# A transformer and expert block on one core: an unused 352-byte tile in the pool of norms

## The chip, the core and the metric

The kernel runs on one core of a Trainium2 chip. The metric is the time of one execution in device microseconds. A core has a matrix engine (TensorE, PE in the profile), a vector engine (DVE), a scalar engine (ACT), GpSimd (POOL), and queues that issue transfers (SP above all). PE reads both operands of a matmul from the on-chip memory SBUF and writes its result to PSUM. One operand, the stationary one, is loaded into the array first (LDWEIGHTS, PEld in the profile); the other, the moving one, is streamed through it column by column (MATMUL). SBUF has 128 partitions; a tile has the same byte address in each of them, so "address" below means the byte in a partition.

## The reference

512 tokens of width 1024 go through two blocks, in float32. What matters here is the first one: four gated feed-forward layers (FFN) with a state-space mixer after the first and a latent attention after the third.

```python
def swiglu(h, w_gate, w_up, w_down):
    return (jax.nn.silu(h @ w_gate) * (h @ w_up)) @ w_down

for i in range(DEPTH):                      # DEPTH = 2
    x = x + 0.5 * swiglu(rms_norm(x, norm_w[i, 0]), ...)
    x = x + (mamba2_mixer if i % 2 == 0 else mla_mixer)(rms_norm(x, norm_w[i, 1]), ...)
    x = x + 0.5 * swiglu(rms_norm(x, norm_w[i, 2]), ...)
```

The hidden width of an FFN is 2816. The second block (a mixer of three kinds of heads, then 16 routed experts) follows on the result.

## The kernel before, in words

All activations lie transposed: a tile is 128 features by 512 tokens, 2048 bytes in each partition. Every float32 value is held as two parts, high and low, in the format float32r, and each product is three matmuls (`mm3`, lines 176 to 181): high weights by high activations (L179), high weights by low activations (L180), low weights by high activations (L181). Names in the profile are `out<-moving,stationary`. With 512 tokens the moving operand has 512 columns, and the stationary one is a block of 128 columns, 512 bytes wide, of a weight tile.

Weights come from memory into two buffers `raw` (9216 bytes each, pool `rawp`), and ACT and DVE split them into `wh` and `wl` (pool `wp`, three buffers of 4608 bytes of each).

An FFN works in two halves of 12 and 10 hidden blocks (`FF_HALVES`). In the gate and up products (`products`, result `ps_p`) the moving operands are `xh` and `xl`, the split norm input, in pool `xw`. The hidden blocks are split into `hh` and `hl` (pool `fact`, line 295), and the down product (`row_matmul`, `row_steps`, result `ps_d`) streams these. The state-space mixer ends in the same `row_steps` with 16 tiles `ghi`/`glo`: the first eight were put into pool `xw` (line 365), the last eight into a pool `shp` of their own (line 374). The attention ends in `row_steps` with tiles `oh`/`ol`, all in `xw`. PE's program is written out by hand (`manual_schedule`); within `row_steps` it takes six matmuls for one result before it goes to the next:

```python
for k in range(2):
    c = slice(k * 512 + d * P, k * 512 + (d + 1) * P)
    f = 2 * u + k
    self.mm3(pd[d], (w[0][:, c], w[1][:, c]), hs[f], f == 0, f == 2 * n - 1)
```

Pools lie one above the other in SBUF in the order in which they are opened. Open from the start of the first block to the end of the mixer are `cst`, `rawp`, `wp`, `xp` (the running sum x), `xw` and `nrm`, whose tiles hold the squares, the row sums and the reciprocal roots of the norms. Each stage opens its own pools above `nrm` and closes them at its end. Pools marked `side="right"` count down from the top, and the pools of the expert stage are opened after `nrm` has been closed. Where the pools named below start in the built programs, in bytes, with the rest after division by 512 in brackets:

| pool | holds | before | after |
|---|---|---|---|
| `cst` | constants; identity at 17632 (224) | 16512 (128) | the same |
| `wp` | `wh`, `wl` | 41888 (416) | the same |
| `xp` | x | 69536 (416) | the same |
| `xw` | `xh`, `xl`, first `ghi`, `glo`, `oh`, `ol` | 85920 (416) | the same |
| `nrm` | `ssq`, `sq`, `dg`, small columns | 118688 (416) | 119040 (256) |
| `fact` | `hh`, `hl` (28 tiles of 2048) | 145472 (64) | 145824 (416) |
| `shp` | last `ghi`, `glo` (16 tiles of 2048) | 157760 (64) | 158112 (416) |
| `st2` | convolved tiles of the mixer (`xT` among them) | 197824 (192) | 198176 (32) |
| `mt3` | attention probabilities | 216064 (0) | 216416 (352) |
| `how` | output weights of the second mixer, from the right | 179232 (32) | the same |
| `et3` | rows of the expert stage | 134048 (416) | the same |

Since the tiles of `wp`, `xw`, `fact` and `shp` are multiples of 512 bytes, the rest in brackets is that of each tile in the pool, and of each weight block.

Of the kernel before, what the change touches and what calls it, by code (L numbers as in the profile page):

```python
# [7 lines left out]
F32 = mybir.dt.float32  # L8
# [10 lines left out]
P = 128  # L19
# [107 lines left out]
class Kern:  # L127
# [10 lines left out]
    def open_features(self, ctx):  # L138

        self.wp = self.pool(ctx, "wp", 3)  # L140
        self.xp = self.pool(ctx, "xp")
        self.xw = self.pool(ctx, "xw")
        self.nrm = self.pool(ctx, "nrm")

    def pool(self, ctx, name, bufs=1, side=None):
        return ctx.enter_context(self.tc.tile_pool(name=name, bufs=bufs, reuse_waits="tile", side=side))
# [2006 lines left out]
```

## Time and profile before

| | |
|---|---|
| median of three runs | 2694.84 us (2693.6 to 2697.28) |
| profiled execution | 2697.9 us, span from first to last instruction 2696.0 us |
| PE busy | 2602.4 us, 97% of the span, 12798 matmuls |
| DVE, ACT, POOL busy | 1553.2, 1059.9, 230.5 us |
| share of PE in the chain that ended last | 86% |
| mean granted PE clock | 0.981 of 2.4 GHz |

Busy times of matmuls overlap: each is recorded from its start to its modelled end, and the next one starts before that. What a matmul costs on a full PE is therefore the distance from its start to the next one's, not its own duration. The profile shows no addresses; those above are read from the programs.

### The profile page before, as it was taken

The numbers are of one execution on the slowest core, as the hardware profiler recorded it, in microseconds if no ns is written. First come the engines' busy times: TensorE is split into PE (matmuls) and PEld (weight loads), VectorE is DVE, ScalarE is ACT, GpSimd is POOL, SyncE is SP. The second block draws the span as 40 slices with busy tenths as digits, with TensorE's granted clock in tenths as the row PEclk, the third lists the DMA queues.
The fourth block names the chain that finished last, engine by engine and source line by source line (L and its number), as shares of the span: only waits on it lengthen the run. The fifth ranks groups of instructions, "written<-read, shape, count | busy, mean of one in ns | idle before, by whom it ended". The sixth has DMA issues, their size and how long they took to land.

```text
span 2696.0 us, 32260 instructions
## 1 busy us (share of the span) xinstructions
PE 2602.4 (97%) x12798; PEld 2144.4 (80%) x12798; DVE 1553.2 (58%) x2609; ACT 1059.9 (39%) x1789; POOL 230.5 (9%) x172
## 2 busy tenths in 40 slices
PE   8999999999999999999999999999999989997996
PEld 6888887888888888888888887888888878766774
DVE  5434357676766454657534367645434364767997
ACT  4322235645443222333322236643322234534674
POOL 0000001111110000000000003200000001303332
PEclk9999998999999999999999999999999989988998
DMA  4222321212134242534422222002222222115796
GB/s 153 94 94 97 106 83 62 79 63 79 63 134 149 102 160 96 183 130 146 167 94 94 94 85 78 17 23 104 94 94 98 106 84 92 48 40 188 254 338 197
DMA packets 57048, 300.77 MB, mean 112 GB/s; under 512 B 12066, under 2 KB 12578, under 8 KB 27706
## 3 DMA queue, kind: packets, MB, share of 16 engines
q1 hardware_dynamic: 49232, 281.21, 29.8%
q0 software_dynamic: 5328, 11.59, 1.5%
q10 hardware_dynamic: 2330, 5.84, 0.6%
q8 instruction: 102, 1.67, 0.2%
q14 instruction: 56, 0.46, 0.0%
HBM read 290.68 MB, written 15.75 MB: 114 GB/s over the span
## 4 chain that ended last, share of the span: by engine, by line
PE 86%; DVE 8%; DMA 3%; ACT 2%; issue 1%; SPq 0%; ACTq 0%; POOL 0%; DVEq 0%; POOLq 0%
PE ps_p L179 12%; PE ps_p L180 12%; PE ps_p L181 12%; PE ps_d L179 8%; PE ps_d L180 8%; PE ps_d L181 8%; PE ps_in L179 3%; PE ps_in L181 3%; PE ps_in L180 3%; DVE wl L167 3%; DMA expert_out<-ey,edst 2%; PE ps_s L833 1%; PE ps_o L859 1%; PE ps_y L541 1%; PE ps_z L180 1%
## 5 line engine op out<-in xcount | busy, mean ns | idle before, releaser
L166 ACT CAST wh<-raw 128x1024 fp32r<-128x1024 f32 (+3 forms) x494 | 485.6, 994 | 1130.7 <-PE ps_p L180 378.3
L167 DVE TENSOR_TENSOR wl<-raw,wh 128x1024 fp32r<-128x1024 f32 (+3 forms) x494 | 574.7, 1175 | 374.6 <-ACT wh L166 365.2
L179 PE MATMUL ps_p<-xh,wh 128*128 128x512 f32 x1408 | 550.2, 391 | 6.7 <-ACT xh L172 6.7
L180 PE MATMUL ps_p<-xl,wh 128*128 128x512 f32 x1408 | 550.0, 391 | 0.6 <-DVE xl L173 0.6
L181 PE MATMUL ps_p<-xh,wl 128*128 128x512 f32 x1408 | 549.4, 390 | 0.0
L179 PEld LDWEIGHTS ps_p<-xh,wh 128*128 128x128 f32 x1408 | 265.6, 189 | 62.7 <-ACT xh L172 6.7
L180 PEld LDWEIGHTS ps_p<-xl,wh 128*128 128x128 f32 x1408 | 265.3, 188 | 57.0 <-DVE xl L173 2.0
L181 PEld LDWEIGHTS ps_p<-xh,wl 128*128 128x128 f32 x1408 | 265.3, 188 | 55.3
L179 PE MATMUL ps_d<-hh,wh 128*128 128x512 f32 x704 | 279.1, 397 | 0.0
L181 PE MATMUL ps_d<-hh,wl 128*128 128x512 f32 x704 | 279.1, 396 | 0.0
L180 PE MATMUL ps_d<-hl,wh 128*128 128x512 f32 x704 | 279.1, 396 | 0.0
L294 DVE TENSOR_TENSOR h<-ps_p,g 128x512 f32<-128x512 f32 x88 | 60.8, 690 | 230.2 <-PE ps_p L181 229.8
L291 DVE TENSOR_TENSOR g<-ps_p,rb 128x512 f32<-128x512 f32 x88 | 60.3, 689 | 177.6 <-PE ps_p L181 177.6
L181 PEld LDWEIGHTS ps_d<-hh,wl 128*128 128x128 f32 x704 | 132.6, 188 | 32.3
L180 PEld LDWEIGHTS ps_d<-hl,wh 128*128 128x128 f32 x704 | 132.6, 188 | 32.3
L179 PEld LDWEIGHTS ps_d<-hh,wh 128*128 128x128 f32 x704 | 132.6, 188 | 32.2
L179 PE MATMUL ps_in<-xh,wh 128*128 128x512 f32 x336 | 140.9, 419 | 0.7 <-ACT wh L166 0.7
L181 PE MATMUL ps_in<-xh,wl 128*128 128x512 f32 x336 | 132.4, 394 | 0.5 <-DVE wl L167 0.5
L180 PE MATMUL ps_in<-xl,wh 128*128 128x512 f32 x336 | 132.1, 393 | 0.0
L181 PEld LDWEIGHTS ps_in<-xh,wl 128*128 128x128 f32 x336 | 63.6, 189 | 15.1 <-DVE wl L167 1.0
L962 DVE SCALAR_TENSOR_TENSOR macc<-mraw,c_act,macc 128x1024 f32<-128x1024 f32 x42 | 53.9, 1284 | 36.8 <-DMA mraw<-w_mod 36.2
L179 PEld LDWEIGHTS ps_in<-xh,wh 128*128 128x128 f32 x336 | 63.9, 190 | 12.9 <-ACT wh L166 1.1
(581 smaller groups left out, 4151.4 us busy)
## 6 DMA issues: line engine op xcount, KB each, us to landing
raw<-w_ffn SPq DMA_DIRECT2D x131, 1024.0 KB
raw<-w_moe SPq DMA_DIRECT2D x48, 1024.0 KB
raw<-w_ssm SPq DMA_DIRECT2D x31, 1024.0 KB
mraw<-w_mod SPq DMA_DIRECT2D x48, 512.0 KB
raw<-w_hyb SPq DMA_DIRECT2D x9, 1024.0 KB
expert_out<-zero SPq DMA_DIRECT2D x8, 512.0 KB
raw<-w_mla SPq DMA_DIRECT2D x4, 1024.0 KB
xtok<-expert_out POOLq DMA_DIRECT2D x8, 512.0 KB, 9.5
```

Source lines behind the costliest of these rows:

```text
L166: a = self.nc.scalar.copy(hi, src)
L167: b = (eng or self.nc.vector).tensor_sub(lo, src, hi.bitcast(F32))
L179: mm(out, ah, bh, start=start, stop=False)
L180: mm(out, ah, bl, start=False, stop=False)
L181: mm(out, al, bh, start=False, stop=stop)
L291: nc.vector.tensor_mul(g, pg, r)
L294: nc.vector.tensor_mul(h, pu, g)
L541: nc.tensor.matmul(py[:, blk(h, 64)], G[h][:, c], xdt[:, 4 * c + h], start=True, stop=True)
L833: nc.tensor.matmul(ps[:, :n], t["qT"][:, blk(i)], t["kT"][:, :n], start=True, stop=False)
L859: nc.tensor.matmul(t["po"][:, blk(i, 64)], t["pT", i][:, blk(j)], v[:, j, h], start=j == 0, stop=j == i)
L962: nc.vector.scalar_tensor_tensor(acc, w, ca[:, k:k + 1], acc, op0=ALU.mult, op1=ALU.add)
```

## The change

One line opens a tile in `nrm` that nothing reads or writes.

```diff
@@ open_features
         self.xp = self.pool(ctx, "xp")
         self.xw = self.pool(ctx, "xw")
         self.nrm = self.pool(ctx, "nrm")
+        self.nrm.tile([P, 88], F32, name="pad")
```

88 float32 are 352 bytes in each partition. The tile is the first that is taken from `nrm`, so it lies at the start of that pool: the other tiles of `nrm` move by 352 bytes too, and so does every pool opened above it while it is open (the pools of the four FFNs, of both mixers and of the modulation). Pools below it, those from the right and those of the expert stage stay where they are. The instructions of the two programs are the same, in the same order, with the same waits, on all five engines; only addresses differ.

## Rows read from the trace of the kernel before

**Rows 1.** The page: engines over the span; the chain by engine and line.

```profile
PE 2602.4 (97%) x12798; PEld 2144.4 (80%) x12798; DVE 1553.2 (58%) x2609; ACT 1059.9 (39%) x1789; POOL 230.5 (9%) x172
...
PE 86%; DVE 8%; DMA 3%; ACT 2%; issue 1%; SPq 0%; ACTq 0%; POOL 0%; DVEq 0%; POOLq 0%
PE ps_p L179 12%; PE ps_p L180 12%; PE ps_p L181 12%; PE ps_d L179 8%; PE ps_d L180 8%; PE ps_d L181 8%; PE ps_in L179 3%; PE ps_in L181 3%; PE ps_in L180 3%; DVE wl L167 3%; DMA expert_out<-ey,edst 2%; PE ps_s L833 1%; PE ps_o L859 1%; PE ps_y L541 1%; PE ps_z L180 1%
```

**Rows 2.** Matmuls by tile: duration min/median/max in ns, first and last start.

```profile
L179 PE MATMUL ps_p<-xh,wh x1408: 387/389/797, 6.7 to 2143.9; 128*128 128x512 f32 x176
...
L179 PE MATMUL ps_d<-hh,wh x704: 392/397/483, 148.9 to 2201.0; 128*128 128x512 f32 x176
...
L180 PE MATMUL ps_d<-hl,wh x704: 392/397/400, 149.1 to 2201.3; 128*128 128x512 f32 x176
...
L179 PE MATMUL ps_d<-ghi,wh x128: 387/394/987, 756.1 to 854.6; 128*128 128x512 f32 x128
...
L179 PE MATMUL ps_d<-oh,wh x64: 389/389/481, 1789.1 to 1835.7; 128*128 128x512 f32 x64
```

**Rows 3.** Windows: engines busy (x instructions touching the window), clock, DMA.

```profile
core 0: us, PE busy (x) PEld busy (x) DVE busy (x) ACT busy (x) POOL busy (x), PEclk, DMA share, GB/s
150.00:216.00 66.00, 66.00 (x283) 53.04 (x283) 23.48 (x27) 12.07 (x12) 0.00 (x0) 1.00 0.23 80
220.00:324.00 104.00, 104.00 (x460) 86.17 (x459) 41.82 (x47) 30.22 (x38) 0.00 (x0) 1.00 0.29 98
789.50:809.50 20.00, 20.00 (x87) 16.09 (x86) 11.95 (x15) 6.15 (x9) 0.00 (x0) 1.00 0.85 307
812.00:832.00 20.00, 20.00 (x90) 16.57 (x89) 16.03 (x17) 7.40 (x10) 0.00 (x0) 1.00 0.63 220
834.50:854.50 20.00, 20.00 (x87) 16.10 (x86) 8.18 (x14) 5.48 (x11) 0.00 (x0) 1.00 0.23 88
1803.00:1836.00 33.00, 33.00 (x147) 27.33 (x146) 17.89 (x27) 13.20 (x22) 0.00 (x0) 1.00 0.28 93
```

**Rows 4.** Timeline of PE: first and last matmul in five of these windows.

```profile
149.81 0.40 PE L180 MATMUL ps_d<-hl,wh 128*128 128x512 f32 x1
...
215.89 0.39 PE L180 MATMUL ps_d<-hl,wh 128*128 128x512 f32 x1
...
219.77 0.39 PE L179 MATMUL ps_p<-xh,wh 128*128 128x512 f32 x1
...
323.81 0.39 PE L179 MATMUL ps_p<-xh,wh 128*128 128x512 f32 x1
...
789.22 0.39 PE L179 MATMUL ps_d<-ghi,wh 128*128 128x512 f32 x1
...
809.37 0.40 PE L181 MATMUL ps_d<-ghi,wl 128*128 128x512 f32 x1
...
811.71 0.39 PE L179 MATMUL ps_d<-ghi,wh 128*128 128x512 f32 x1
...
831.88 0.39 PE L181 MATMUL ps_d<-ghi,wl 128*128 128x512 f32 x1
...
1802.79 0.40 PE L181 MATMUL ps_d<-oh,wl 128*128 128x512 f32 x1
...
1835.89 0.39 PE L180 MATMUL ps_d<-ol,wh 128*128 128x512 f32 x1
```

**Rows 5.** Waits: who waited for whom, us in total, times, longest us.

```profile
ACT wh L166 <- PE ps_d L180: 344.4, 92, 8.8
```

**Rows 6.** Matmuls with the identity as moving operand, by tile, columns as in rows 2.

```profile
L1540 PE MATMUL ps_hT<-squares,hg x120: 270/272/328, 2497.0 to 2646.5; 128*128 128x128 f32 x120
L845 PE MATMUL ps_pT<-squares,prb x112: 270/273/330, 1673.1 to 1792.9; 128*128 128x128 f32 x112
L511 PE MATMUL ps_x<-squares,xT x64: 270/272/273, 442.0 to 759.5; 128*128 128x128 f32 x64
```

**Rows 7.** Output product of the second mixer, by tile, columns as in rows 2.

```profile
L179 PE MATMUL ps_out<-ow,yh x32: 389/396/483, 2427.5 to 2460.4; 128*128 128x512 f32 x32
```

**Rows 8.** Span and mean granted clock of the core.

```profile
core 0: 2696.0 us, clock 0.981
```

## The prediction

> **What bounds the kernel now.** The page comes first: PE is busy for 97% of the span, and 86% of the chain that ended last is PE [rows 1]. Products of one form, 128x512 float32r, fill most of it: by line the chain is ps_p three times 12% and ps_d three times 8%. A change that moves only addresses can change the time in two ways, by what a single instruction takes or by who meets whom at a memory, and on this kernel either must show on PE to count.
>
> So the second view is the tiles. All 1408 x 3 products ps_p have a median of 389 ns [rows 2]. The FFN's down products stream the same 512 columns against the same weight tiles, and have 397 ns (704 x 3 of them). The attention's output product, which runs through the same `row_steps` lines as these, has 389 ns. The state-space mixer's, through `row_steps` again, has 394 ns, which lies between. The code that issues them is not what makes 397 of 389.
>
> Durations overlap, so the third view gives the distance from start to start: windows in which PE never pauses, with the count of matmuls that touch them [rows 3], and the first and last of these on the timeline [rows 4]. In the FFN's down product 283 matmuls make 282 steps from 149.81 to 215.89 us: 66.08 / 282 = 234.3 ns. In the following up product 459 steps from 219.77 to 323.81 give 226.7 ns. In the attention's output 146 steps from 1802.79 to 1835.89 give 226.7 ns. The granted clock is 1.00, that is 2.4 GHz, in all of them.
>
> The mixer's output decides what the difference hangs on. By the order of `row_steps` each of its two quarters takes 96 matmuls on the eight tiles in `xw`, then 96 on the eight in `shp`. The window 789.5 to 809.5 lies on `shp`: 86 steps in 20.15 us, 234.3 ns. The window 812 to 832 lies on `xw`: 89 steps in 20.17 us, 226.6 ns. The window 834.5 to 854.5 lies on `shp` again, with the count of the first, 87 against 90. One stage, one set of lines, one clock, three windows, and the step follows the pool of the moving tile. It does not follow the load: DMA moved 307, 220 and 88 GB/s in the three, and DVE and ACT were busier in the second than in the others [rows 3].
>
> What differs between the pools is their start. Weights and `xw` have the rest 416 after division by 512; `fact` and `shp` have 64. Every 512-column product above at 226 to 227 ns has operands with equal rests; those at 234 ns have a distance of 160 between them (64 - 416 + 512).
>
> **The change, part by part.** No instruction is added, removed or moved past another, so there is no queue or wait to price, only addresses.
>
> Tiles of `fact` and `shp` go from 64 to 416, the rest of the weights that they meet. The FFNs have 704 x 3 = 2112 such matmuls. The mixer has 128 x 3 = 384, half of them, 192, on `shp`. Each should take 226.7 in place of 234.3 ns: 2112 x 7.6 ns = 16.1 us, and 192 x 7.6 ns = 1.5 us, together 17.5 us. From below the gain is bounded by nothing at all (if the rest is not what counts), from above by this sum, since no 512-column stretch that I timed runs under 226.6 ns. I take the whole sum, because two windows already show `row_steps` at 226.6 and 226.7 ns when the rests agree, and after the change the relation is the same one.
>
> Does it reach the end? In these windows PE is busy without a gap (66.00 of 66.00, 20.00 of 20.00), and ps_d is 24% of the chain. The next thing that could be late is weights. ACT waits for ps_d 92 times, 344.4 us in all, for a weight buffer to come free [rows 5]; it stands ahead of PE. A pair of split weight tiles feeds 24 matmuls in the up product as in the down product, and the up product holds 226.7 ns over 104 us with 98 GB/s of transfers and no gap [rows 3]. The down product then asks for the same rate, so the cover suffices.
>
> The tiles of `nrm` move too, from 416 to 256. They feed PE in 14 products that spread a norm over the rows and in some sums of one column; at the 7.6 ns seen above the 14 would cost 0.1 us. I take nothing.
>
> The remaining products with one moved operand are mostly transposes: about 620 whose moving operand is the identity, which stays, while the turned tile moves. Those of `hg` (rest 416), `prb` (0) and `xT` (192) have medians of 272, 273 and 272 ns [rows 6]. Three rests give one duration, so I take nothing; if each lost 7.6 ns it would be 4.7 us. Products of which both operands move keep their distance. DVE, ACT and POOL have slack in the stages that I sum, and the transfers into moved tiles feed work beside them. I take nothing for these either.
>
> The sum is -17.5 us. The profiled execution took 2697.9 us, which is 3.1 us above the median of the three runs; it goes to 2680.4, and the median from 2694.8 to **2677.3 us**. The three runs differ by 3.7 us, and the mean clock of 0.981 [rows 8] says that some stretches run at 1.2 GHz; an earlier end of a stage can make such a stretch a little longer or shorter. For the likeliest case alone I therefore give 2672 to 2683.
>
> **The rivals.** First, nothing changes: 2694.8 us. The address table allows another reading of the same rows: every moving tile at 227 ns lies below byte 118688 and every one at 234 above 145000. If the place counts and not the rest, `fact` and `shp` stay as high as they are and keep their 234 ns. One row leans against it, without force: the `how` tiles lie at 179232 and up, as high, with the rest 32, and their product has 396 ns in one of its three lines, broken up by other work [rows 7]. It would also come out so if the second operand cost nothing at any address and something else in the two pools held them back. The Trainium skill speaks for no change: SBUF — State Buffer, section "Who interferes with whom", has it that PE never waits on anyone for SBUF, and TensorE: Matmul & The Clock Gate, section "Step-by-step: what each phase is for", says "Loading the next tile's weights doesn't steal SBUF read bandwidth from the running matmul." By these pages an address costs nothing and the sum is zero; the two windows of one stage, 234.3 and 226.6 ns, do not agree with that. I give this rival 7 in 100.
>
> Second, half the gain: rests by a larger number than 512 count as well, and only part of the blocks meet well. The tiles of `fact` have 416 by 2048 then, those of `xw` 1952. Against it: in ps_p the eight weight blocks of a tile lie 512 bytes apart, so eight distances by 2048 and more occur, and the window of 104 us has one step throughout. The time would be about 2686. I give 4 in 100.
>
> Third, slower. Moved tiles start at a multiple of 64 bytes before and 32 bytes past one after. If a moving operand wants a start at a multiple of 64 and `xw` is fast for another reason, the down products get worse. The row of `hl` shows 400 ns as the longest [rows 2], 3 ns above the median; a step that grew by as much on 2304 matmuls would give 6.9 us, and with half of what the transposes could lose at the utmost some 9: about 2704. It decides the sign once the mean step in these stretches passes 236.6 ns (5.4 us over 2304). Against it stand the 4224 matmuls ps_p, which start 32 past a multiple of 64 and are the fastest. I give 4 in 100.
>
> **How the numbers follow.** The likeliest case has 85 in 100. What three runs can tell from no change is about 0.2%, 5.4 us. The likeliest and the half gain are faster by more: 0.89. The first rival is the same: 0.07. The third is slower: 0.04. The range reaches from just under the likeliest case to past the half gain, 2671 to 2688; outside it are the first and third rivals and a little of the likeliest, under 2 in 10.
>
> **What would show it.** In the profile after, the median of `hh` and `hl` falls from 397 to 389 ns, and that of `ghi` from 394 to 389. A gapless 66 us of the FFN's down product is touched by some 292 matmuls in place of 283. The three windows on the mixer's output have the same count. Each FFN's first down half (288 matmuls) is 2.2 us shorter, its second (240) 1.8 us, and the up products, the attention and the experts take what they took. I am wrong if the step of the down product stays at 234 (then the place counts, or what is in the pools), or if it falls and the end does not come earlier, by a new gap on PE or more time at 1.2 GHz.

## The result and the profile after

The changed kernel takes 2676.11 us (median of 6 runs, 2673.09 to 2677.55), the kernel before 2694.68 us on the same chip (median of 6). The ratio is 0.9934, 95% interval 0.9923 to 0.9945. That is 18.6 us less, where 17.5 were forecast (2677.3 us), and lies inside the range of 2671 to 2688.

The page of the profiled execution after the change (2677.55 us, span 2675.6) begins and ends its chain with these lines. They answer to [rows 1]; all line numbers of the code have grown by one.

```profile
PE 2580.3 (96%) x12798; PEld 2139.8 (80%) x12798; DVE 1552.2 (58%) x2609; ACT 1060.3 (40%) x1789; POOL 229.2 (9%) x172
...
PE 86%; DVE 9%; ACT 2%; DMA 1%; issue 1%; SPq 0%; ACTq 0%; POOL 0%; DVEq 0%
PE ps_p L180 12%; PE ps_p L182 12%; PE ps_p L181 12%; PE ps_d L180 8%; PE ps_d L181 8%; PE ps_d L182 8%; DVE wl L168 3%; PE ps_in L180 3%; PE ps_in L182 3%; PE ps_in L181 3%; PE ps_s L834 1%; PE ps_o L860 1%; PE ps_y L542 1%; PE ps_z L181 1%; PE ps_z L180 1%
```

The same 12798 matmuls keep PE busy for 22.1 us less, and DVE, ACT and POOL have not moved by more than 1.3 us. The same products lead the chain; the transfer `expert_out<-ey,edst`, 2% of it before, is no longer in this line. It belongs to the expert stage, behind everything that the sum counted.

The second view is the matmuls by tile, with minimum, median and maximum of the duration in ns, and the first and last start; it answers to [rows 2].

```profile
L180 PE MATMUL ps_p<-xh,wh x1408: 387/389/794, 6.8 to 2127.5; 128*128 128x512 f32 x176
...
L180 PE MATMUL ps_d<-hh,wh x704: 388/389/481, 148.6 to 2182.8; 128*128 128x512 f32 x176
...
L181 PE MATMUL ps_d<-hl,wh x704: 389/389/390, 148.8 to 2183.1; 128*128 128x512 f32 x176
...
L180 PE MATMUL ps_d<-ghi,wh x128: 387/389/987, 750.7 to 848.3; 128*128 128x512 f32 x128
...
L180 PE MATMUL ps_d<-oh,wh x64: 387/389/478, 1774.9 to 1821.5; 128*128 128x512 f32 x64
```

`hh`, `hl` and `ghi` have come down to the 389 ns that `xh` and `oh` had all along. The last start in a row is a clock for the whole of what was summed: all FFNs and the state-space mixer lie before the last `ps_d<-hh`. It started at 2201.0 us before [rows 2] and starts at 2182.8 now, 18.2 us earlier.

The third view is the windows, engines busy (x instructions touching the window), granted clock and DMA; it answers to [rows 3].

```profile
148.50:214.00 65.50, 65.50 (x291) 54.24 (x290) 24.63 (x28) 13.37 (x14) 0.00 (x0) 1.00 0.25 88
218.00:322.00 104.00, 104.00 (x461) 86.11 (x460) 41.82 (x47) 30.22 (x38) 0.00 (x0) 1.00 0.29 99
...
785.00:805.00 20.00, 20.00 (x90) 16.56 (x89) 12.31 (x16) 6.81 (x10) 0.00 (x0) 1.00 0.88 311
807.00:827.00 20.00, 20.00 (x89) 16.54 (x89) 16.42 (x17) 7.33 (x9) 0.00 (x0) 1.00 0.63 225
829.50:849.50 20.00, 20.00 (x90) 16.58 (x89) 8.70 (x18) 6.71 (x14) 0.00 (x0) 1.00 0.20 70
```

The down product of the first FFN half is gapless still (65.50 of 65.50), and 291 matmuls now touch a window that is half a microsecond shorter than the one that 283 touched. The up product behind it is as it was. In the three windows on the mixer's output the counts were 87, 90, 87; they are 90, 89, 90. The first and the last of the 288 matmuls of that down half, on PE's timeline:

```profile
148.57 0.39 PE L180 MATMUL ps_d<-hh,wh 128*128 128x512 f32 x1
...
213.62 0.39 PE L182 MATMUL ps_d<-hh,wl 128*128 128x512 f32 x1
```

287 steps in 65.05 us are 226.7 ns each, where [rows 4] gave 234.3.

### The profile page after: what moved, and what is told of

It reads as the page before. It is cut to its first block, busy times and chain, and to the rows that moved or that the text cites. A ratio compares the mean times of both kernels' runs of the same rounds, so it can differ in the third digit from the quotient of the medians.

```text
span 2675.6 us, 32260 instructions
## 1 busy us (share of the span) xinstructions
PE 2580.3 (96%) x12798; PEld 2139.8 (80%) x12798; DVE 1552.2 (58%) x2609; ACT 1060.3 (40%) x1789; POOL 229.2 (9%) x172
## 4 chain that ended last, share of the span: by engine, by line
PE 86%; DVE 9%; ACT 2%; DMA 1%; issue 1%; SPq 0%; ACTq 0%; POOL 0%; DVEq 0%
PE ps_p L180 12%; PE ps_p L182 12%; PE ps_p L181 12%; PE ps_d L180 8%; PE ps_d L181 8%; PE ps_d L182 8%; DVE wl L168 3%; PE ps_in L180 3%; PE ps_in L182 3%; PE ps_in L181 3%; PE ps_s L834 1%; PE ps_o L860 1%; PE ps_y L542 1%; PE ps_z L181 1%; PE ps_z L180 1%
## 5 line engine op out<-in xcount | busy, mean ns | idle before, releaser
L181 PE MATMUL ps_p<-xl,wh 128*128 128x512 f32 x1408 | 549.6, 390 | 0.6 <-DVE xl L174 0.6
L181 PEld LDWEIGHTS ps_p<-xl,wh 128*128 128x128 f32 x1408 | 265.3, 188 | 57.5 <-DVE xl L174 2.2
L181 PE MATMUL ps_d<-hl,wh 128*128 128x512 f32 x704 | 273.9, 389 | 0.0
L181 PEld LDWEIGHTS ps_d<-hl,wh 128*128 128x128 f32 x704 | 132.2, 188 | 27.4
L181 PE MATMUL ps_in<-xl,wh 128*128 128x512 f32 x336 | 131.3, 391 | 0.0
```

The lines of the kernel that those rows point to most:

```text
L181: mm(out, ah, bl, start=False, stop=False)
```

## The experiments

All kernels below issue the same instructions in the same order on each engine as the kernel before; they differ in addresses. Steps are distances between the starts of neighbouring matmuls on PE's timeline, as a mean over all of a kind that run without a pause. "Distance" is the start of the moving tile less that of the weight block, after division by 512.

**Only what lies above the norms moves.** The change also moves the tiles of `nrm`. Here the 352 bytes lie in a pool of their own above it, so that `nrm` stays.

```diff
         self.nrm = self.pool(ctx, "nrm")
+        self.pool(ctx, "padp").tile([P, 88], F32, name="padp")
```

> The 352 bytes stand in a pool of their own above the pool of norms, whose tiles stay at their old addresses; fact and shp start with the rest 416 as in the changed kernel. If the distance between moving tile and weights is the whole cause: ratio 0.993, about 2676 us, and a step of 226.7 ns in the down products. If the move of the norms' own tiles brought or cost a part: a ratio between 0.994 and 1.000, or under 0.992.

Measured: 2673.63 us, ratio 0.9932 (0.9915 to 0.9948), step of `ps_d<-hh` 226.6 ns.

```profile
L180 PE MATMUL ps_d<-hh,wh x704: 389/389/481, 148.3 to 2180.9; 128*128 128x512 f32 x176
```

The whole effect is there without the norms' own tiles.

**Everything from the weights up moves by 96 bytes.** Absolute places and remainders change, distances do not.

```diff
+        self.pool(ctx, "padp").tile([P, 24], F32, name="padp")
         self.wp = self.pool(ctx, "wp", 3)
```

> 96 bytes stand ahead of the weight pool, so that weights, xw, fact and shp all rise by 96: rests 0, 0, 160, 160. Every distance is that of before. If the distance counts: ratio 1.000, about 2695 us, ps_d<-hh 234.3 ns a step and ps_p 226.7. If the start of the moving tile alone counts (416 is good because it is 32 past a multiple of 64): the tiles of xw, at a multiple of 64 now, fall to about 234 (some 5600 matmuls, +40 us) and fact, 32 past one, rises to 227 (-17.5 us): about 2717 us.

Measured: 2693.78 us, ratio 1.000 (0.9991 to 1.001). The tile view of this kernel has the durations of before:

```profile
L180 PE MATMUL ps_p<-xh,wh x1408: 387/389/792, 6.6 to 2144.0; 128*128 128x512 f32 x176
...
L180 PE MATMUL ps_d<-hh,wh x704: 392/397/482, 148.8 to 2201.1; 128*128 128x512 f32 x176
```

Weights and `xw` start at a multiple of 512 here, `fact` and `shp` at 160 past one, and the two products keep their steps of 226.8 and 234.3 ns. Neither kind of start has a value by itself, which takes away the rival of starts at a multiple of 64.

**The fast tiles are moved off the weights.** 160 bytes ahead of `xw` give it the distance that `fact` had. 352 more above `nrm` keep `fact` and `shp` at 160.

```diff
         self.xp = self.pool(ctx, "xp")
+        self.pool(ctx, "padx").tile([P, 40], F32, name="padx")
         self.xw = self.pool(ctx, "xw")
         self.nrm = self.pool(ctx, "nrm")
+        self.pool(ctx, "padp").tile([P, 88], F32, name="padp")
```

> 160 bytes ahead of xw and 352 after it: xw has the rest 64 against 416 of the weights, fact and shp have 64 as before. If the distance counts, the products on xw get the step that fact had: ps_p 234.3 ns in place of 226.7 for 4224 matmuls, ps_in, the mixer's and the attention's outputs on xw for some 1400 more: +40 us, about 2735, ratio 1.015; ps_d<-hh keeps 234.3. If the 234 ns belong to the tiles of fact and shp for another reason than their start: ratio 1.000.

Measured: 2729.98 us, ratio 1.0141 (1.0124 to 1.0158), 35.6 us slower than before. The tile view (two lines of code are added, so L179 is L181 here), and a window of 62 us on a down product and one of 100 us on an up product:

```profile
L181 PE MATMUL ps_d<-hh,wh x704: 392/397/475, 152.2 to 2234.3; 128*128 128x512 f32 x176
...
L181 PE MATMUL ps_p<-xh,wh x1408: 391/397/792, 6.7 to 2177.2; 128*128 128x512 f32 x176
...
L181 PE MATMUL ps_d<-oh,wh x64: 392/397/481, 1813.2 to 1860.9; 128*128 128x512 f32 x64
```

```profile
153.00:215.00 62.00, 62.00 (x267) 49.83 (x266) 21.61 (x25) 11.30 (x12) 0.00 (x0) 1.00 0.25 86
220.00:320.00 100.00, 100.00 (x429) 80.39 (x428) 40.26 (x46) 27.79 (x35) 0.00 (x0) 1.00 0.29 98
```

`xw` still lies low, below 119 KB, and its products now have the 397 ns and the step of 234.3 ns of the down product. That is the end of the rival by which the place decides.

**The weights move instead.** `hh` keeps the remainder 64 that it had before; the weights come to it.

```diff
+        self.pool(ctx, "pada").tile([P, 40], F32, name="pada")
         self.wp = self.pool(ctx, "wp", 3)
+        self.pool(ctx, "padb").tile([P, 88], F32, name="padb")
         self.xp = self.pool(ctx, "xp")
         self.xw = self.pool(ctx, "xw")
```

> 160 bytes ahead of the weight pool and 352 behind it: the weights go from the rest 416 to 64; xw, fact and shp rise by 512 and keep their rests 416, 64 and 64. If the distance counts: ps_d<-hh falls to 226.7 ns though its tiles' rests have not changed (-17.5 us), and ps_p, now at a distance of 352, rises to somewhere between 229 and 238 ns (+10 to +60 us): a ratio of 0.998 to 1.016. If the moving tile's start alone counts: 226.7 and 234.3 ns stay with their tiles, ratio 1.000.

Measured: 2706.95 us, ratio 1.0056 (1.0039 to 1.0072).

```profile
L181 PE MATMUL ps_d<-hh,wh x704: 387/389/481, 150.7 to 2211.3; 128*128 128x512 f32 x176
...
L181 PE MATMUL ps_p<-xh,wh x1408: 392/392/792, 6.7 to 2155.9; 128*128 128x512 f32 x176
L183 PE MATMUL ps_p<-xh,wl x1408: 389/399/632, 8.0 to 2156.4; 128*128 128x512 f32 x176
```

The moving tiles of the down product lie where their remainder was slow, and their step is 226.7 ns, because the weights have the same remainder now. The products on `xw`, at a distance of 352, have lost: 233.0 ns on `xh`, 234.0 on `xl`. One part of the kernel gains and the larger part loses more.

**All distances in steps of 32 bytes.** In the next four kernels only the pools of the FFNs are raised, in each FFN by another amount, so that one run shows four distances. The edit, here with the amounts of the second (192, 224, 256, 288):

```diff
+            self.ffns = getattr(self, "ffns", -1) + 1
+            pad = (8, 16, 24, 32)[self.ffns]
+            if pad:
+                self.pool(ctx, "fpad", 1).tile([P, pad], F32, name="fpad")
             nrm = self.pool(ctx, "fnrm", 1)
```

> Only the pools of the four FFNs are raised, by another amount in each: in the order of the FFNs the tiles of fact stand 32, 64, 96 and 128 bytes past the rest of the weights (by 512). If only equal rests are good: 229 to 238 ns a step in all four. If the step grows with the distance: near 227 at 32, 234 at 128. If equality by 32 or 64 bytes is enough: 226.7 at 64 and 128, or at all four.

> As the one before, with distances of 192, 224, 256 and 288. If only equal rests by 512 are good: 229 to 238 ns in all four. If equality by 256, 128 or 64 bytes is enough: 226.7 at 256.

> As the one before, with distances of 320, 352, 384 and 416. If only equal rests by 512 are good: 229 to 238 ns in all four. If there is a better distance than 0, one of these or of the neighbouring runs shows a step under 226.6 ns.

> Distances of 448 and 480, and as controls in the same execution 0 (third FFN) and 160 (fourth, as in the kernel before). Controls: 226.7 and 234.3 ns. The others: 229 to 238 ns if only equal rests by 512 are good.

Measured, one run of each: 2688.04, 2686.82, 2690.06 and 2686.0 us, before on the same chip 2694.81. A window of 62 us in the first down half of each of the four FFNs, in the kernel with 32, 64, 96 and 128:

```profile
150.00:212.00 62.00, 62.00 (x267) 49.86 (x266) 21.75 (x24) 10.66 (x11) 0.00 (x0) 1.00 0.25 85
990.00:1052.00 62.00, 62.00 (x272) 50.90 (x271) 25.50 (x29) 13.46 (x14) 0.00 (x0) 1.00 0.26 90
1357.00:1419.00 62.00, 62.00 (x268) 49.87 (x267) 21.23 (x24) 10.51 (x10) 0.00 (x0) 1.00 0.26 85
1964.00:2026.00 62.00, 62.00 (x267) 49.90 (x266) 21.03 (x24) 10.51 (x10) 0.00 (x0) 1.00 0.25 85
```

The same windows in the kernel with 192, 224, 256 and 288:

```profile
150.00:212.00 62.00, 62.00 (x267) 49.72 (x266) 21.99 (x24) 10.90 (x11) 0.00 (x0) 1.00 0.25 86
990.00:1052.00 62.00, 62.00 (x268) 49.90 (x267) 25.03 (x27) 12.90 (x13) 0.00 (x0) 1.00 0.28 100
1357.00:1419.00 62.00, 62.00 (x275) 51.38 (x274) 22.34 (x25) 11.43 (x12) 0.00 (x0) 1.00 0.26 87
1964.00:2026.00 62.00, 62.00 (x268) 49.78 (x267) 21.89 (x24) 10.78 (x11) 0.00 (x0) 1.00 0.25 85
```

The counts 272 and 275 stand out, at the distances 64 and 256. The two controls in the kernel with 448 and 480, 0 in its third FFN and 160 in its fourth:

```profile
1357.00:1419.00 62.00, 62.00 (x276) 51.34 (x275) 22.39 (x25) 11.11 (x12) 0.00 (x0) 1.00 0.24 85
1964.00:2026.00 62.00, 62.00 (x266) 49.87 (x265) 21.48 (x24) 10.52 (x10) 0.00 (x0) 1.00 0.25 85
```

Mean steps of `ps_d` from the starts, two parts `hh` to one `hl`, in ns:

| distance by 256 | 0 | 32 | 64 | 96 | 128 | 160 | 192 | 224 |
|---|---|---|---|---|---|---|---|---|
| first half of the 512 (0 to 224) | 226.7 | 233.3 | 229.0 | 233.4 | 233.1 | 234.3 | 233.3 | 233.3 |
| second half (256 to 480) | 226.7 | 233.3 | 229.0 | 233.4 | 233.3 | 234.3 | 233.3 | 233.3 |

The two rows are one within 0.2 ns: the pattern has a period of 256 bytes, not of 512. No distance in these steps of 32 is better than 0. The distance of the kernel before, 160, is the worst of the eight. The kernel with the weights moved agrees from other tiles: its distance of 352 is 96 by 256, and its 233.0 and 234.0 ns are 233.3 in the mean of two parts `xh` to one `xl`, where the table has 233.4.

**256 as well as 0, in the whole kernel.** The line of the change with 24 floats.

```diff
+        self.nrm.tile([P, 24], F32, name="pad")
```

> The same line as the change with 24 floats, 96 bytes in place of 352: fact and shp rise to the rest 160 by 512, a distance of 256 from the weights. Theory A, the distance counts by 256: step of ps_d<-hh 226.7 ns, hh median 389 ns, about 2676 to 2677 us, ratio 0.993 to the kernel before, as the change. Rival B, only a distance of 0 by 512 is free in this pool, and the one FFN of the sweep that showed 226.5 ns at 256 was fast for another reason: 233 to 234 ns, ratio 0.999 to 1.000.

Measured: 2675.98 us, ratio 0.9921 (0.9908 to 0.9934). 96 bytes do what 352 do. The row of `hh` and the down-product window that had 267 matmuls in the kernel with `xw` moved:

```profile
L180 PE MATMUL ps_d<-hh,wh x704: 389/389/481, 148.2 to 2180.7; 128*128 128x512 f32 x176
```

```profile
153.00:215.00 62.00, 62.00 (x275) 51.36 (x274) 23.51 (x27) 12.65 (x12) 0.00 (x0) 1.00 0.25 85
```

**A distance in between.** The same line with 40 floats, distance 320.

```diff
+        self.nrm.tile([P, 40], F32, name="pad")
```

> The same line with 40 floats, 160 bytes: distance 320, which is 64 by 256. The sweep showed a mean step of about 229 ns there in one FFN. Theory A (the loss is read off the table of distances by 256): 2304 matmuls gain 234.3 - 229 = 5.3 ns each, 12.2 us, about 2682.5 us, ratio 0.9955. Rival B, a distance either fits or doesn't (all or nothing): 2677 us, ratio 0.9934, or 2694 us, ratio 1.000.

Measured: 2678.52 us (6 runs, 2677.5 to 2687.1), ratio 0.9946 (0.9932 to 0.9961).

```profile
L180 PE MATMUL ps_d<-hh,wh x704: 388/394/475, 148.4 to 2187.0; 128*128 128x512 f32 x176
```

```profile
153.00:215.00 62.00, 62.00 (x272) 50.88 (x271) 22.63 (x25) 12.27 (x12) 0.00 (x0) 1.00 0.25 85
```

The time by itself can't tell the expected 0.9955 from the 0.9934 of the rival that knows only fit or no fit: the interval holds both. The trace can. The step is 230.4 ns on `hh` and 226.1 on `hl`, 229.0 in the mean, and the last `ps_d<-hh` starts at 2187.0 us: 14.0 us earlier than before, where the change has 18.2 and this table gives 2304 x 5.3 = 12.2. A loss comes in sizes. The 1.8 us beyond the table are no more than the clock can give: ahead of that start the trace's record of the granted clock has 23.9 us at 1.2 GHz where before has 30.7, and 6.8 us at half the clock are worth up to 3.4, an estimate. The runs at an equal mean clock say the same. At 0.983 the kernel before took 2690.47 us, with 40 floats 2677.81 and 2677.85 (12.6 less), with 24 floats 2672.11 and 2672.56 (18.1 less); at 0.982 they took 2695.14, 2685.17 (10.0 less) and 2676.31 (18.8 less). The larger difference of the medians, 17.1 us, holds this difference of clocks too.

## Why the prediction was right, point by point

**The step.** It falls from 234.3 to 226.7 ns in the FFNs and in the `shp` half of the mixer, as predicted, and the counts show it: `hh` and `hl` have a median of 389 ns, `ghi` too, and the three windows of the mixer agree within one matmul. That it is the distance of the two operands, and neither of them alone, is shown from three sides: moving both by 96 bytes changes nothing (ratio 1.000), moving the fast tiles off the weights makes them slow (ratio 1.0141), moving the weights to the slow tiles makes these fast.

**The sum.** 17.5 us were summed. The last `ps_d<-hh`, which has all 2304 products before or beside it, starts 18.2 us earlier, and 18.6 us came in the medians. Of the 0.7 us that the start has beyond the sum, 0.3 lie ahead of the first down product (the first `ps_d<-hh` starts at 148.9 us before [rows 2] and at 148.6 after); the rest is not settled. Kernels with equal steps differ by more: that start lies at 2182.8, 2180.9 and 2180.7 us in the change and in the kernels that move only the pools above the norms or use 96 bytes. Ahead of it the first has 30.7 us at 1.2 GHz and the other two 27.3; 3.4 us at half the clock are worth up to 1.7, an estimate that is most of the difference.

**The span.** It fell by 20.4 us between the two profiled executions, 2.2 more than that start did. The stretch behind the last down product (the second mixer and the experts) is 494.5 us long before, and 492.3 after. It is not the change that shortens it: with everything 96 bytes higher and the old steps it takes from 2201.6 to 2693.5, 491.9 us. The prediction had left this open by the runs' own spread, and that was the right size for it.

**The cover.** Weights arrive in time. ACT's wait for a buffer behind the down product, [rows 5], became this, and PE has no gap in the window of 65.50 us:

```profile
ACT wh L167 <- PE ps_d L181: 329.4, 89, 8.5
```

**What was taken as nothing.** The norms' own tiles: 2673.63 us without moving them against 2676.11 with, and the intervals of the ratios overlap. The transposes on the identity ([rows 6]) still have 272 or 273 ns in the median, though the tiles `prb` (remainder 0 before, 352 now) and `xT` (192 before, 32 now) moved and of the three only `hg` stayed:

```profile
L1541 PE MATMUL ps_hT<-squares,hg x120: 270/272/308, 2475.3 to 2625.1; 128*128 128x128 f32 x120
L846 PE MATMUL ps_pT<-squares,prb x112: 272/273/331, 1658.9 to 1778.6; 128*128 128x128 f32 x112
L512 PE MATMUL ps_x<-squares,xT x64: 271/273/421, 436.4 to 754.8; 128*128 128x128 f32 x64
```

A duration is not a cost, and the prediction read durations alone here. The steps bear it out: the median from start to start is 109 ns for each of the three, before and after.

**The rivals.** "Nothing changes" rested on the place of the pools, and the kernel with `xw` moved has slow tiles below 119 KB. The two statements of the Trainium skill that the prediction weighed (SBUF — State Buffer, section "Who interferes with whom", and TensorE: Matmul & The Clock Gate, section "Step-by-step: what each phase is for") don't hold when they are taken for PE's own two reads: with the same instructions and only other addresses the ratio goes from 0.9921 to 1.0141, and the measurement decides. Whether another engine can make PE wait was not tried. "Half the gain" by a larger number than 512 fell with the change itself. "Slower" by starts at a multiple of 64 fell with the 96 bytes under everything.

**Where it was finer than the chip.** The prediction spoke of equal rests by 512. That was enough and more than is needed: 256 is the number, and a quarter of it, 64, loses only some 2.3 ns of the 7.6 (three quarters, 192, lose 6.6). Two distances were all that the trace of before offered in long gapless stretches, so it could not be told there; the forecast didn't hang on it.

**Where an experiment's size was off.** With `xw` moved 40 us were expected and 35.6 came. The steps are as expected, 234.3 ns in all three lines of `ps_p`. The rest goes with the clock. At an equal mean clock of 0.984 the kernel before took 2688.51 and 2690.90 us and this one 2729.22, 2729.82 and 2730.13: 40.0 us between the means. The traces agree. The last `ps_d<-hh` starts at 2234.3 us here and at 2201.1 in the kernel with 96 bytes under everything, which has the old steps, 33.2 us apart; ahead of it PE was granted 1.2 GHz for 17.1 us here and for 30.7 there. 13.6 us at half the clock are worth up to 6.8, an estimate, and 33.2 + 6.8 = 40.0. The kernel with the weights moved has the same 17.1 us. Both have slow products on `xw`; why less time at 1.2 GHz goes with them is not settled.

## What to carry to other kernels

Where PE is full of pairs of a weight load and a 512-column product, compare the start-to-start step of products of one shape over the stages; if they differ at one granted clock, look at the addresses of the moving tile and of the weight block by 256 bytes. Place every pool whose tiles meet the same weights at the same remainder as these; a few unused bytes do it, and any later edit of a pool that lies between them can undo it, so the remainder wants to be held by the code and not by chance. Judge such an edit by the step and by the start of the last product of the kind, since the time of one run moves by itself with the granted clock: the thirteen runs of the kernel before that go with the first experiments lie between 2687.95 and 2697.77 us.

## What the runs showed of the hardware

The step of a float32r product of 128x512 depends on the distance of the addresses of its two operands by 256 bytes, from 226.7 ns (0) over 229.0 (64) to 234.3 (160), and not on either address alone. That the two reads hinder each other is the reading that fits; no view shows the reads themselves, and which part of the memory or of the engine is held in common no run here shows. The steps at a bad distance aren't even: at 160 they go 231, 234, 235, 234, 231, 238, 237 ns and begin again, seven steps with a mean of 234.3, while the products come in threes. It goes on within 1 ns through the 282 steps of the first window of [rows 3], of whose 66 us DVE was busy for 23.48 and ACT for 12.07, so it does not come and go with what these two read and write. At 64 the high activations take 230.4 where the low ones take 226.0. Neither the transposes of 128 columns (a step of 109 ns at every distance seen) nor DVE and ACT (busy 1552.2 and 1060.3 us after, 1553.2 and 1059.9 before) answer to the addresses in a way that these runs can see. For the transposes that says little: 109 ns are nearly twice the 56.7 that a quarter of 226.7 would be, so something else may set their pace and hide a loss.
